# Ten of the sixteen k tiles of an input projection by Strassen's scheme, ahead of the rest

## The chip, the cores and the metric

The kernel runs on one core of a Trainium2 chip. Its engines work side by side: TensorE (PE) multiplies matrices into PSUM, VectorE (DVE) and ScalarE (ACT) do elementwise work and read PSUM, GpSimd (POOL) does elementwise work in SBUF alone, SyncE (SP) issues most of the DMAs. The metric is the device time of one execution in microseconds (us).

## The reference

One decoder layer for a prompt of 1024 tokens and 8 samples of one token each, all in float32:

```python
h = rmsnorm(x, g_norm) * (1 + scale) + shift        # shift, scale, gate from silu(c) @ w_ada
p = h @ w_in                                        # 2048 -> 5 * 1024 + 8 + 3 * 1024
q, k, v, o, z_ml, i_pre, f_pre, u, v_cm, z_cm = split(p)
h_ml = rmsnorm(sigmoid(o) * mlstm(q, k, v, i_pre, f_pre)) * silu(z_ml)      # 4 heads of 256, chunks of 128 tokens
h_cm = gelu(u) * spatial_mix(layernorm(gelu(v_cm))) * silu(z_cm)            # 4 groups of 256
y = rmsnorm(x + gate * (concat(h_ml, h_cm) @ w_out), g_final)
```

Outputs are y for prompt and samples, the new matrix memories, normalisers and maxima, and the normalised v rows of the samples.

## The kernel before

The 1024 tokens are worked in two halves of 512. The input projection (2048 features in, 16 k tiles of 128) is cut into 32 sections of 256 columns: eight keys (k, v, q, o, z, vc, u, zc) for each of four heads j, so that every section runs once in each half. Each float32 operand is split into a high and a low part, and a product takes three matmuls: high by high, low by high, high by low. `wsplit` (L318) splits the weights, a cast on ACT (L324) and a subtraction on DVE (L325), a piece of two k tiles at a time; it does so in each half anew. `section` (L395) runs the matmuls: with tokens on the PSUM partitions for v, o and vc (L426, L427, L429, 256 columns), with features on the partitions for the others (L437, L440; 512 columns in the second half, 256 and 264 in the first, where the samples' eight columns ride behind the tokens). In the first half the samples' part of v, o and vc is a product of its own (`sample_mm`, L334).

`take` (L367) loads the weight pieces, one `stream` of pieces planned in order (`plan`, L377), some pieces ahead into a ring of three `raw` buffers, and splits them into rings of four. Work that needs no place of its own (the samples' gates, state update and output `s_out` L1112, the ada gate, the first half's `finish` L824) is cut into steps; `run` (L454) puts one step after every second piece of a section, four to a section. The steps of `s_out` load w_out again in pieces of 512 KB (L1134) and multiply them by the samples' rows (L1136). `fold_x` (L808) adds x and the gate to the second half's sums in steps, behind the last vc section; what is left of the background steps is drawn there first, ahead of the u of the last head (L1337 to L1339).

The order within an engine is the program's where `late` (the framework's hold) stands; elsewhere the framework's scheduler orders the instructions by its own model of when they are ready. Each engine then executes its list in order.

At the start the ada weights of 256 features at a time (`ada_pair`, L152), x of the first half (L1219) and the pieces of k, v and q come in turns, so that the first three sections grow k tile by k tile (L1246 to L1275). h of the second half is prepared beside the last section of the first. Of a head: k is evicted and transposed (`ml_k`, L568, transposes L581), then v, q, the chunk recurrence `ml_chain` (L623), o, z, `ml_post` (L659), vc, the output projection of the head (`out_proj`, L797), u, zc.

## Time and profile before

| | |
|---|---|
| median of 3 runs | 2187.31 us (2184.13 to 2187.61) |
| span of the profiled execution, first to last instruction | 2186.8 us |
| PE busy with matmuls | 2125.5 us (97%), 14290 instructions |
| DVE / ACT / POOL busy | 1052.9 / 694.3 / 283.6 us |
| moved by DMA | 307.84 MB, mean 141 GB/s |

The profiled execution has no time of its own beside its span; the span lies 0.5 us below the median of the runs. A busy time counts the duration of instructions; matmuls overlap their successors, so a matmul's duration is longer than what it adds to the time, and prices are better read from start to start. In the rows of instructions in order of time, the columns are start, duration, engine, line, output and inputs, count; a bracket at the end gives the idle time ahead of the instruction and what ended it.

### The profile page before, as it was taken

The page shows a single profiled execution, that of the slowest core. Times are in us where ns is not written, and L with a number is a line of the kernel's source. Part 1 is how long each engine was busy: PE and PEld are TensorE (multiplying, and loading weights), DVE is VectorE, ACT ScalarE, POOL GpSimd, SP SyncE. Part 2 cuts the span into 40 slices and gives each one's busy share as a digit, 9 for nine tenths or more (in the row PEclk, how much of TensorE's full clock was granted, in tenths as well). Part 3 has the DMA queues.
Part 4 walks back from the last instruction along what each step waited for, and adds up shares of the span by engine and source line. Part 5 has one row for each costly group of instructions (what it writes and reads, how often), then busy time and mean ns, then how long its engine had stood idle before and what let it go on. Part 6 is the DMA issues. An engine that isn't in the chain of part 4 may idle for free. (4 is left out here: it accounts for less than half of the span.)

```text
span 2186.8 us, 35645 instructions
## 1 busy us (share of the span) xinstructions
PE 2125.5 (97%) x14290; PEld 1823.1 (83%) x14290; DVE 1052.9 (48%) x2078; ACT 694.3 (32%) x1342; POOL 283.6 (13%) x322
## 2 busy tenths in 40 slices
PE   5999999999999999999999999999999999999996
PEld 3778898888988989889978898788888787788985
DVE  4344634325343354433556556655754335344396
ACT  2233232223223423223262353333332232322324
POOL 1100010000100000000040551100010000001064
PEclk8999999999999999999999999999999999999998
DMA  9962343444535433222342454565563353544343
GB/s 335 323 203 71 109 149 113 135 139 129 153 111 177 129 99 97 79 68 84 100 144 79 143 168 134 165 182 167 182 188 102 118 159 112 168 135 120 92 149 122
DMA packets 280550, 307.84 MB, mean 141 GB/s; under 512 B 16160, under 2 KB 250800, under 8 KB 279872
## 3 DMA queue, kind: packets, MB, share of 16 engines
q1 hardware_dynamic: 276288, 296.49, 44.2%
...
q8 instruction: 112, 1.84, 0.3%
...
HBM read 285.18 MB, written 20.32 MB: 140 GB/s over the span
## 5 line engine op out<-in xcount | busy, mean ns | idle before, releaser
L325 DVE TENSOR_TENSOR wlo<-raw,whi 128x512 fp32r<-128x512 f32 x634 | 458.8, 729 | 901.1 <-ACT whi L324 347.1
L324 ACT CAST whi<-raw 128x512 fp32r<-128x512 f32 x634 | 385.2, 620 | 1234.3 <-PE pp L440 370.8
L437 PE MATMUL pp<-hhi,whi 128*128 128x256 f32 (+1 forms) x1856 | 518.1, 330 | 0.4 <-DVE hhi L258 0.4
L440 PE MATMUL pp<-hlo,whi 128*128 128x256 f32 (+1 forms) x1856 | 509.4, 325 | 0.4 <-DVE hlo L263 0.4
L426 PE MATMUL pp<-whi,hhi 128*128 128x256 f32 x1536 | 380.4, 287 | 0.0
L427 PE MATMUL pp<-whi,hlo 128*128 128x256 f32 x1536 | 372.7, 281 | 0.0
L437 PEld LDWEIGHTS pp<-hhi,whi 128*128 128x128 f32 x1856 | 310.3, 188 | 63.7 <-issue 28.5
L437 PE MATMUL pp<-hhi,wlo 128*128 128x256 f32 (+1 forms) x1856 | 352.9, 324 | 0.0
L440 PEld LDWEIGHTS pp<-hlo,whi 128*128 128x128 f32 x1856 | 310.7, 188 | 30.4 <-issue 0.8
L426 PEld LDWEIGHTS pp<-whi,hhi 128*128 128x128 f32 x1536 | 290.6, 189 | 24.6 <-issue 22.2
L437 PEld LDWEIGHTS pp<-hhi,wlo 128*128 128x128 f32 x1856 | 279.6, 188 | 32.2 <-issue 0.8
L427 PEld LDWEIGHTS pp<-whi,hlo 128*128 128x128 f32 x1536 | 290.4, 189 | 0.8 <-issue 0.4
L429 PE MATMUL pp<-wlo,hhi 128*128 128x256 f32 x1536 | 213.6, 282 | 0.0
L791 PE MATMUL pp<-whi,g 128*128 128x512 f32 x488 | 193.9, 397 | 5.0 <-ACT g L687 5.0
L429 PEld LDWEIGHTS pp<-wlo,hhi 128*128 128x128 f32 x1536 | 195.1, 189 | 0.0
L792 PE MATMUL pp<-whi,g 128*128 128x512 f32 x488 | 192.9, 395 | 0.2 <-DVE g L689 0.2
L806 DVE TENSOR_TENSOR yacc<-yacc,pp 128x512 f32<-128x512 f32 x204 | 136.3, 684 | 41.8 <-PE pp L794 41.5
L794 PE MATMUL pp<-wlo,g 128*128 128x512 f32 x488 | 154.0, 396 | 1.1 <-DVE wlo L325 1.0
L791 PEld LDWEIGHTS pp<-whi,g 128*128 128x128 f32 x488 | 92.0, 189 | 27.8 <-ACT g L687 5.8
L794 PEld LDWEIGHTS pp<-wlo,g 128*128 128x128 f32 x488 | 92.1, 189 | 23.4 <-DVE wlo L325 2.1
L792 PEld LDWEIGHTS pp<-whi,g 128*128 128x128 f32 x488 | 92.0, 189 | 21.1 <-DVE g L689 0.5
L819 POOL TENSOR_TENSOR yacc<-yacc,xl 128x512 f32<-128x512 f32 x32 | 53.4, 1683 | 77.3 <-DVE yacc L818 76.5
...
## 6 DMA issues: line engine op xcount, KB each, us to landing
raw<-in_w_in_dram SPq DMA_DIRECT2D x256, 512.0 KB
...
```

What stands on the lines that cost most here:

```text
L324: hold(A.copy(hi, raw))
L325: hold(V.tensor_tensor(out=lo, in0=raw, in1=hi.bitcast(F32), op=ALU.subtract))
L426: pin(T.matmul(o, hhi[kt][:, tk], hi, start=(st and tt % 2 == 0), stop=False, skip_group_check=True))
L427: pin(T.matmul(o, hlo[kt][:, tk], hi, start=False, stop=False, skip_group_check=True))
L429: pin(T.matmul(o, hhi[kt][:, tk], lo, start=False, stop=en, skip_group_check=True))
L437: pin(T.matmul(o, w[:, fk], hhi[kt][:, tk], start=so, stop=en, skip_group_check=True))
L440: pin(T.matmul(o, hi[:, fk], hlo[kt][:, tk], start=False, stop=False, skip_group_check=True))
L791: T.matmul(po, hc[a][0][:, tk], sp_[a][0][:, 0, :], start=(start and a == 0), stop=False)
L792: T.matmul(po, hc[a][1][:, tk], sp_[a][0][:, 0, :], start=False, stop=False)
L794: T.matmul(po, hc[a][0][:, tk], sp_[a][1][:, 0, :], start=False, stop=(a == 1 and not more))
L806: V.tensor_tensor(out=yv, in0=yv, in1=po, op=ALU.add)
L819: G.tensor_tensor(out=yv, in0=yv, in1=xl[:, t2, :], op=ALU.add)
```

## The change

For 10 of the 16 k tiles the input projection is now done first, for all 1024 tokens, by the Strassen-Winograd scheme. A block is two k tiles by two halves of the tokens (four parts of h) and two halves of a section's columns (four parts of the weights). Seven products of sums of these parts replace eight products of the parts. `combos` forms the seven operands of h of a block, each split into high and low; `Seven` forms the weight operands of a section (four sums on POOL), splits them and runs the products into four PSUM banks, which ACT, DVE and POOL add up to the four output parts. This runs in two stretches over all 32 sections: stretch 1 with blocks 0 and 1 (4 k tiles), stretch 2 with blocks 2 to 4 (6 k tiles). The sums go to DRAM (`spool`), stretch 2 reads those of stretch 1 and adds to them. In the background of stretch 1 h of blocks 2 to 4 is prepared, in that of stretch 2 the ada weights of blocks 5 to 7, h of the first half of them, and the ada gate.

Then the halves run as before over the 6 k tiles that are left, all sections with features on partitions; `part` loads the sums of a section from DRAM (512 KB) and DVE adds them when it evicts PSUM. `tokens` turns v, o and vc on TensorE. The samples' products for the 10 k tiles run in stretches 1 and 2, two sections at a time (`sample_two`); for the 6 others they ride behind the tokens in all sections of the first half. Weight pieces of the halves are half as large (one piece of two k tiles, or one k tile of w_out), six loads are in flight and three pieces split ahead. A section now has three pieces, and a background step follows each. `s_out` takes its pieces from the ring `part`. At the start x is read whole, all eight token tiles, and the ada weights of blocks 0 and 1 follow. Buffers are opened and closed by phase. The diff, cut to its core:

```diff
-SPLIT = ["v0", "v1", "v2", "v3", "o0", "o1", "o2", "o3", "vc0", "vc1", "vc2", "vc3", "k0", "q0"]
+KEYS = ("k", "v", "q", "o", "z", "vc", "u", "zc")
+SECS = [(key, j) for j in range(NH) for key in KEYS]
+SUBS = [(0, 2), (2, 3)]
+K2 = 2 * sum(n for _, n in SUBS)
+KN = KT - K2
...
+    spool = [[dr.tile([P, 2048], F32, name=f"spool{n}_{i}") for i in range(len(SECS))] for n in range(len(SUBS))]
+    psd = [dr.tile([P, len(SECS) * 256], F32, name=f"psd{n}") for n in range(len(SUBS))]
...
+    def combos(at, hf, eng):
+        a11, a21, a12, a22 = hf
+        def put(n, t):
+            A.copy(at[:, n, :], t)
+            V.tensor_tensor(out=at[:, 7 + n, :], in0=t, in1=at[:, n, :].bitcast(F32), op=ALU.subtract)
+        put(0, a11)
+        put(1, a12)
+        put(2, a22)
+        yield
+        t1, t2 = s2(), s2()
+        V.tensor_tensor(out=t1, in0=a21, in1=a22, op=ALU.add)
+        eng.tensor_tensor(out=t2, in0=t1, in1=a11, op=ALU.subtract)
+        put(3, t1)
+        put(4, t2)
+        yield
+        t3 = s2()
+        V.tensor_tensor(out=t3, in0=a12, in1=t2, op=ALU.subtract)
+        put(6, t3)
+        yield
+        t4 = s2()
+        eng.tensor_tensor(out=t4, in0=a11, in1=a21, op=ALU.subtract)
+        put(5, t4)
+        yield
+    def slot(pool):
+        return pool.tile([P, 14, 512], F32R, tag="as", name=nm("as"), bufs=3 if pool is pl["big"] else 1)
+    class Seven:
+        def __init__(self, sub, n):
+            self.sub, self.n = sub, n
+            b0, self.nb = SUBS[sub]
+            key, j = SECS[n]
+            c0 = SEC[key] + j * 256
+            self.raw = pl["big"].tile([P, 2 * self.nb, 256], F32, tag="raw", name=nm("raw"), bufs=2)
+            S.dma_start(self.raw, win[:, 2 * b0:2 * b0 + 2 * self.nb, c0:c0 + 256])
+            self.co = None
+        def load_co(self):
+            self.co = cot()
+            if self.sub:
+                S.dma_start(self.co.rearrange("p a b -> p (a b)"), spool[self.sub - 1][self.n])
+        def sums(self):
+            r = self.raw.rearrange("p (b i) (n c) -> p b i n c", i=2, n=2)
+            b11, b12, b21, b22 = r[:, :, 0, 0, :], r[:, :, 0, 1, :], r[:, :, 1, 0, :], r[:, :, 1, 1, :]
+            t = [pl["big"].tile([P, self.nb, P], F32, tag="t", name=nm("t"), bufs=4) for _ in range(4)]
+            sub = lambda o, a, b: G.tensor_tensor(out=o, in0=a, in1=b, op=ALU.subtract)
+            sub(t[0], b12, b11)
+            sub(t[1], b22, t[0])
+            sub(t[2], b22, b12)
+            sub(t[3], t[1], b21)
+            self.prod = [(b11, 0, 0), (t[1], 4, 1), (b21, 1, 0), (t[0], 3, 2), (t[2], 5, 1), (b22, 6, 2), (t[3], 2, 3)]
+            self.hl = {}
+        def split(self, m):
+            w = self.prod[m][0]
+            hi, lo = (pl["big"].tile([P, self.nb, P], F32R, tag=t, name=nm(t), bufs=4) for t in ("hi", "lo"))
+            A.copy(hi, w)
+            V.tensor_tensor(out=lo, in0=w, in1=hi.bitcast(F32), op=ALU.subtract)
+            self.hl[m] = (hi, lo)
+        def product(self, m, at):
+            _, place, bank = self.prod[m]
+            if m == 0:
+                self.ps = [None] * 4
+            first = self.ps[bank] is None
+            if first:
+                self.ps[bank] = psb()
+            o = self.ps[bank]
+            hi, lo = self.hl.pop(m)
+            nb = self.nb
+            for b in range(nb):
+                for n, (w, d) in enumerate(((hi, 0), (hi, 7), (lo, 0))):
+                    T.matmul(o, w[:, b, :], at[b][:, place + d, :], start=(first and b == 0 and n == 0), stop=(b == nb - 1 and n == 2), skip_group_check=True)
+            x, y, z, v = self.ps
+            co = self.co
+            c11, c21, c12, c22 = co[:, 0, 0:512], co[:, 0, 512:], co[:, 1, 0:512], co[:, 1, 512:]
+            add = lambda e, o, a, b, op=ALU.add: e.tensor_tensor(out=o, in0=a, in1=b, op=op)
+            half = lambda t: pl["big"].tile([P, 512], F32, tag=t, name=nm(t), bufs=2 if t == "pa" else 1)
+            if m == 0:
+                self.a = half("pa")
+                A.copy(self.a, x)
+            elif m == 1:
+                self.u = half("pu")
+                add(V, self.u, self.a, y)
+                if self.sub:
+                    add(G, c12, c12, self.u)
+            elif m == 2:
+                if self.sub:
+                    add(V, c11, c11, x)
+                else:
+                    A.copy(c11, x)
+            elif m == 3:
+                if self.sub:
+                    add(V, c22, c22, z)
+                else:
+                    A.copy(c22, z)
+            elif m == 4:
+                add(V, self.a, self.a, y)
+                if self.sub:
+                    add(G, c21, c21, self.a)
+                add(V if self.sub else G, c22, c22, self.a)
+            elif m == 5:
+                add(V, c12, c12 if self.sub else self.u, z)
             else:
+                add(V, c21, c21 if self.sub else self.a, v, ALU.subtract)
+        def store(self):
+            S.dma_start(spool[self.sub][self.n], self.co.rearrange("p a b -> p (a b)"))
+    def sample_two(sa, sb):
+        ps = psb()
+        b0, nb = SUBS[sa.sub]
+        nk = 2 * nb
+        for i in range(nk):
+            j = i % 4
+            for n, s in enumerate((sa, sb)):
+                T.matmul(ps[32 * j:32 * j + 32, 256 * n:256 * n + 256], hs[:, 2 * b0 + i, :], s.raw[:, i, :],
+                         start=(i < 4 and n == 0), stop=(i + 4 >= nk), tile_position=(0, 32 * j), skip_group_check=True)
+        e = s2()
+        A.copy(e, ps)
+        S.dma_start(psd[sa.sub][:, sa.n * 256:sa.n * 256 + 512], e)
+    def sub_phase(sub, at, bg):
+        secs = {}
+        def get(n):
+            if n < len(SECS) and n not in secs:
+                secs[n] = Seven(sub, n)
+        AHEAD = 3
+        get(0)
+        get(1)
+        secs[0].sums()
+        for m in range(AHEAD):
+            secs[0].split(m)
+        for n in range(len(SECS)):
+            s = secs[n]
+            s.load_co()
+            for m in range(7):
+                if m == 3 and n + 1 < len(SECS):
+                    secs[n + 1].sums()
+                g = m + AHEAD
+                if g < 7:
+                    s.split(g)
+                elif n + 1 < len(SECS):
+                    secs[n + 1].split(g - 7)
+                if m == 1 and n % 2 == 0:
+                    sample_two(s, secs[n + 1])
+                s.product(m, at)
+                next(bg, None)
+            s.store()
+            get(n + 2)
+            del secs[n]
...
+    def part(key, h, half):
+        if (key, h, half) not in parts:
+            t = pl["wp"].tile([P, 2, 512], F32, tag="part", name=nm("part"), bufs=2)
+            late(S.dma_start(t, spool[-1][SECS.index((key, h))].rearrange("p (f t) -> p f t", f=2)[:, :, half * 512:half * 512 + 512]))
+            parts[key, h, half] = t
+        return parts[key, h, half]
+    def section(key, h, half):
+        samples = half == 0
         pt = [psb(), psb()]
+        hv = hh[half]
+        fm = part(key, h, half)
+        if samples:
+            acc = psb()
+            cols = [[(pt[0][:, 0:256], slice(0, 256)), (pt[1][:, 0:256 + NB], slice(256, HALF + NB))],
+                    [(pt[0][:, 256:512], slice(0, 256)), (acc[:, 0:256 + NB], slice(256, HALF + NB))]]
         else:
+            cols = [[(pt[ft], slice(0, HALF))] for ft in range(2)]
+        for q in range(KN // 2):
+            hi2, lo2 = take("s", key, h, q, half)
+            for ps_ in range(2):
+                for g in range(2):
+                    kt = 2 * q + g
+                    hi, lo = hi2[:, g, :], lo2[:, g, :]
+                    st, en = (kt == 0 and ps_ == 0), (kt == KN - 1 and ps_ == 1)
+                    for ft in range(2):
+                        fk = slice(ft * P, ft * P + P)
+                        for n, (o, tk) in enumerate(cols[ft]):
+                            so = st and not (samples and n == 0 and ft == 1)
+                            w = hi if ps_ == 0 else lo
+                            T.matmul(o, w[:, fk], hv[:, kt, 0, tk], start=so, stop=en, skip_group_check=True)
+                        if ps_ == 0:
+                            for o, tk in cols[ft]:
+                                T.matmul(o, hi[:, fk], hv[:, kt, 1, tk], start=False, stop=False, skip_group_check=True)
+            if q < KN // 2 - 1:
+                yield None
+        n = SECS.index((key, h)) + 1
+        if half == 0 or n < len(SECS):
+            part(*SECS[n % len(SECS)], half + n // len(SECS))
+        if samples:
+            collect(key, h, [cols[ft][1][0][:, 256:] for ft in range(2)])
+        ts = []
+        for ft in range(2):
+            t = g2([P, 512])
+            for o, tk in cols[ft]:
+                tk = slice(tk.start, min(tk.stop, HALF))
+                V.tensor_tensor(out=t[:, tk], in0=o[:, 0:tk.stop - tk.start], in1=fm[:, ft, tk], op=ALU.add)
+            ts.append(t)
+        yield ts
...
+    def tokens(ts):
+        pt = [psb(), psb()]
+        for tt in range(4):
+            for ft in range(2):
+                c = (tt % 2) * 256 + ft * P
+                T.transpose(pt[tt // 2][:, c:c + P], ts[ft][:, tt * P:tt * P + P], ident)
+        return pt
...
-    def run(key, h, token_major, half, mid=None):
-        for i, r in enumerate(section(key, h, token_major, half == 0)):
-            if i == 3 and mid is not None:
-                mid()
-            if i % 2 == 1:
-                next(bgq[0], None)
+    def run(key, h, half):
+        for r in section(key, h, half):
+            next(bgq[0], None)
         return r
...
-                    raw = wp.tile([P, 4, 256], F32, tag="raw", name=nm("raw"), bufs=3)
+                    raw = pl["wp"].tile([P, 4, 256], F32, tag="part", name=nm("raw"), bufs=2)
...
     def back_a():
         yield from s_gates()
-        for key in ("k", "v", "q"):
-            yield from sample_only(key, 0)
-        for n in range(4):
-            yield from ada_gate(n)
-        part = sm([P, 4, 4])
-        for tt in range(4):
-            for n in range(2):
-                xl = wp.tile([P, 1024], F32, tag="xl", name=nm("xl"), bufs=2)
-                late(S.dma_start(xl, xp[:, 4 + tt, n * 1024:n * 1024 + 1024]))
-                yield
-                for i in range(2):
-                    late(A.activation(xl[:, i * 512:i * 512 + 512], xl[:, i * 512:i * 512 + 512], AF.Square, accum_out=part[:, tt, 2 * n + i:2 * n + i + 1]))
-        rstdB[0] = rstd_rows(part)
-        yield
+        yield from h_second(1, G)
...
+    at = []
+    for blk in range(SUBS[0][1]):
+        for _ in ada_pair(blk, True):
+            pass
+        hf = hf_tile()
+        for _ in h_block(blk, lambda tt: xk[:, tt, blk * 256:blk * 256 + 256], [0, 1], hf):
+            pass
+        at.append(slot(pl["s1" if blk else "big"]))
+        for _ in combos(at[-1], hf, V):
+            pass
+    nxt = {}
+    def bg_a():
+        b0, nb = SUBS[1]
+        for blk in range(b0, b0 + nb):
+            yield from ada_pair(blk)
+        for blk in range(b0, b0 + nb):
+            xl = [load_x(blk, 0), load_x(blk, 1)]
+            yield
+            nxt["hf"] = hf_tile()
+            yield from h_block(blk, lambda tt: xl[tt // 4][:, tt % 4, :], [0, 1], nxt["hf"])
+            if blk < b0 + nb - 1:
+                t = slot(pl["big"])
+                nxt[blk] = t
+                yield from combos(t, nxt["hf"], G)
+    def bg_b():
+        for blk in range(K2 // 2, 8):
+            yield from ada_pair(blk)
+        yield from h_second(0, V)
         for n in range(4):
+            yield from ada_gate(n)
+    bg = bg_a()
+    sub_phase(0, at, bg)
+    for _ in bg:
+        pass
+    close_pool("s1")
+    open_pool("hh0", "left")
+    b0, nb = SUBS[1]
+    t = slot(pl["big"])
+    for _ in combos(t, nxt["hf"], V):
+        pass
+    bg = bg_b()
+    sub_phase(1, [nxt[b] for b in range(b0, b0 + nb - 1)] + [t], bg)
+    for _ in bg:
+        pass
+    close_pool("pre")
+    open_pool("w2", "left")
...
+            ks = run("k", j, half)
             if half == 0 and j == 0:
                 def front():
                     yield from gates(0)
+                for _ in front():
                     pass
                 bgq[0] = back_a()
+            k, ktok = ml_k(ks)
+            if pend is not None:
+                out_proj(*pend, half)
+                pend = None
+            v = ml_v(tokens(run("v", j, half)))
+            gt = gst["gt"]
+            Pm = w_intra(j, gt)
+            q = run("q", j, half)
+            num = ml_chain(half, j, k, ktok, v, q, Pm, gt)
+            o = ml_o(tokens(run("o", j, half)))
+            z = ml_z(run("z", j, half), j)
+            hc = ml_post(j, num, o, z, gt)
+            y = cm_v(tokens(run("vc", j, half)))
             out_proj(ya, 2 * j, hc, half, first=(j == 0), ns=3 + (j < 3 or half == 0))
             hml = hc
             m = cm_mix(j, y)
...
                 if half:
                     bgq[0] = fold_x(ya, half)
                     next(bgq[0])
+            cm_u(run("u", j, half), m)
...
```

## Rows read from the trace of the kernel before

**Rows 1.** the page's busy line and its 40 slices of PE, in tenths

```profile
PE 2125.5 (97%) x14290; PEld 1823.1 (83%) x14290; DVE 1052.9 (48%) x2078; ACT 694.3 (32%) x1342; POOL 283.6 (13%) x322
...
PE   5999999999999999999999999999999999999996
```

**Rows 2.** waits of PE: who waited for whom; us in total, times, longest

```profile
PE pp L252 <- DVE x_a L1259: 11.1, 1, 11.1
...
PE pp L581 <- ACT g L573: 3.6, 4, 2.0
```

**Rows 3.** busy time by stretch: length, engines busy, granted clock, DMA share, GB/s

```profile
40.00:50.00 10.00, 9.06 (x71) 5.50 (x64) 9.13 (x29) 0.63 (x2) 0.72 (x1) 1.00 1.09 375
300.00:1100.00 800.00, 795.48 (x6122) 720.09 (x6121) 327.46 (x605) 231.14 (x466) 50.06 (x66) 1.00 0.39 117
1150.00:2100.00 950.00, 937.64 (x5403) 792.65 (x5402) 494.58 (x1018) 311.54 (x564) 127.00 (x141) 0.99 0.47 140
```

**Rows 4.** PE in order of time: start, us, line; ends of two pieces

```profile
1502.20 0.28 PE L426 MATMUL pp<-whi,hhi 128*128 128x256 f32 x1
...
1505.05 0.28 PE L426 MATMUL pp<-whi,hhi 128*128 128x256 f32 x1
...
1507.85 0.40 PE L437 MATMUL pp<-hhi,whi 128*128 128x512 f32 x1
...
1510.63 0.40 PE L437 MATMUL pp<-hhi,whi 128*128 128x512 f32 x1
```

**Rows 5.** PE in order of time, from 1688 us: transposes, section, s_out

```profile
1688.48 1.16 PE L1124 MATMUL pp<-ident,g 8*128 8x8 f32 x16
1689.56 0.39 PE L426 MATMUL pp<-whi,hhi 128*128 128x256 f32 x1
...
1690.38 0.28 PE L426 MATMUL pp<-whi,hhi 128*128 128x256 f32 x1
1690.59 0.64 PE L1136 MATMUL pp<-raw,hs 128*32 128x256 f32 x8
1691.16 0.39 PE L427 MATMUL pp<-whi,hlo 128*128 128x256 f32 x1
```

**Rows 6.** PE in order of time, from 1288 us: eight transposes, next section

```profile
1288.66 1.03 PE L680 MATMUL pp<-ident,g 128*128 128x128 f32 x8
1289.45 0.37 PE L426 MATMUL pp<-whi,hhi 128*128 128x256 f32 x1
```

**Rows 7.** PE in order of time: the first product of the input projection

```profile
40.67 0.50 PE L437 MATMUL pp<-hhi,whi 128*128 128x512 f32 x1 [0.38 <-DVE hhi L258]
```

**Rows 8.** groups by line, DVE and POOL, shapes apart: busy us, mean ns

```profile
L806 DVE TENSOR_TENSOR yacc<-yacc,pp 128x512 f32<-128x512 f32 x204 | 136.3, 684 | 41.8 <-PE pp L794 41.5
L1069 DVE SCALAR_TENSOR_TENSOR r<-xl,g 128x256 f32<-128x256 f32 x64 | 23.8, 425 | 11.8 <-DMA g<-psf 6.1 <-DMA g<-psa 5.5
...
L648 POOL TENSOR_SCALAR r<-g,s 128x257 f32<-128x257 f32 x32 | 31.5, 994 | 229.4 <-PE pp L642 120.0 <-ACT g L601 53.2 <-DVE r L1069 42.8
L263 POOL TENSOR_TENSOR hlo<-g,hhi 128x512 fp32r<-128x512 f32 x16 | 20.8, 1325 | 17.6 <-ACT hhi L260 17.6
```

**Rows 9.** POOL and DVE in order of time, from 1270 us

```profile
1270.00 10.37 POOL L836 TENSOR_TENSOR yacc<-yacc,gt 128x512 f32<-128x512 f32 x7 [1.22 <-ACT yacc L835]
...
1271.69 3.31 DVE L325 TENSOR_TENSOR wlo<-raw,whi 128x512 fp32r<-128x512 f32 x2
```

**Rows 10.** DVE in order of time: products of s_state with q

```profile
1520.10 0.43 DVE L1069 SCALAR_TENSOR_TENSOR r<-xl,g 128x256 f32<-128x256 f32 x1 [4.14 <-DMA g<-psf]
```

**Rows 11.** SP, ACT, PE in order of time: load, first use, s_out's end

```profile
1703.36 0.37 SPq L353 DMA_DIRECT2D raw<-in_w_in_dram  x1
...
1707.54 0.62 ACT L324 CAST whi<-raw 128x512 fp32r<-128x512 f32 x1 [1.36 <-DMA raw<-in_w_in_dram]
...
1969.11 0.64 PE L1136 MATMUL pp<-raw,hs 128*32 128x256 f32 x8
```

656 lines of the change are left out of this document (242 added, 414 removed).

## The prediction

> **What bounds the kernel now.** I read the page's busy line and its slices first [rows 1]: TensorE (PE) is busy 97% of the span, in all slices but the first and the last; VectorE (DVE) 48%. The waits of PE say the same [rows 2]: the longest is 11.1 us at the start, and the transposes of k behind their eviction wait 3.6 us in all. So the time is the sum of PE's instructions at the pace at which they issue, plus a start and an end. The windows [rows 3] give the slack: in 300 to 1100 us, at full clock, PE is busy 99.4% with DVE at 41%; in 1150 to 2100 us 98.7% with DVE at 52%. Matmul durations overlap, so a matmul is priced from start to start [rows 4]: 24 of 256 columns take 2.85 us (0.1188 each), 12 of 512 columns 2.78 us (0.2317).
>
> **The matmuls of the input projection.** Removed: 24 token-major sections of 192 x 0.1188 = 547; 18 sections of the first half with the samples' columns, 192 x 0.1188 = 411; 22 feature-major ones of 96 x 0.2317 = 489; sum 1447 us. Added: stretch 1 (4 k tiles), 32 sections x 7 products x 2 blocks x 3 x 0.2317 = 311; stretch 2 (6 k tiles) 32 x 7 x 3 x 3 x 0.2317 = 467; the 6 k tiles left over, first half 32 x 72 x 0.1188 = 274, second half 32 x 36 x 0.2317 = 267; sum 1319. Net -128 us: 102 from seven products for eight (32 sections x 5 blocks x 1536 columns at 2.4 GHz), the rest from 512-column matmuls and fewer sample columns.
>
> **PE work that is added.** Sample matmuls rise from 448 to 640 instructions; 8 take 0.57 us [rows 5], so 192 x 0.071 = +14. sample_two puts two sections on one column group in succession; if that costs the overlap between groups, up to +36. v, o and vc now come with features on partitions and are turned by tokens(): 24 x 8 = 192 transposes; 8 take 0.79 us [rows 6], +19. PE's net so far: -95 us.
>
> **The start: +15 (0 to +35).** Before, the first product starts at 40.67 us [rows 7], and from 40 to 50 us PE is at 91% with the DMAs at 375 GB/s [rows 3]. Now all 8 MB of x and the ada weights of two blocks (8 MB) come ahead of the first product: 16 MB at that rate is 43 us, behind about 7 us of small loads. Then come transposes, the first combinations (eleven DVE instructions of about 0.68 [rows 8]) and their waits, some 15 us: about 65 us. PE does about 10 us more useful work before that point than it did, hence +15.
>
> **Joints: +18 (5 to 35).** The fifth block's combinations take the buffer of a block of stretch 1 and can't be written before that stretch ends: +6. Where the halves begin, w_s is loaded and turned at once, and gates(0) is run to its end behind the first k section, where the o and z sections covered it before: +12.
>
> **Waits for evictions: +12 (0 to 36).** tokens() waits for two DVE additions of 0.68 [rows 8], where the transposes of k waited for one ScalarE copy, up to 2.0 us [rows 2]. I take 24 x 0.5, since PE does take later matmuls first: seven of the next piece stand ahead of s_out's L1136 while its transposed rows are copied [rows 5]. Without that, 24 x 1.5.
>
> **DVE and GpSimd in stretches 1 and 2: +25 (10 to 60).** By section in stretch 1: seven splits of 256 elements (0.42, as L1069) and four additions from PSUM (0.68, as L806) make 5.7 us on DVE; on GpSimd four sums of 256 (0.74, scaled down from L263's 1.33 for 512) and one of 512 make 4.3 [rows 8]. Stretch 2: 7 x 0.56 + 7 x 0.68 = 8.7 on DVE, 4 x 1.0 + 2 x 1.3 = 6.6 on GpSimd. The two get in each other's way [rows 9]: while seven GpSimd instructions ran in 10.37 us, two DVE subtractions took 3.31 us in place of 1.4, so 58% of GpSimd's time was lost to DVE. With that DVE needs 8.2 of PE's 10.3 us in stretch 1 (9.73 + 0.57 of samples) and 12.6 of 15.5 in stretch 2: 80%, where the trace of before knows 41 and 52%. PE's idle share doubled between those two (0.6 to 1.3%); carried on it is about 3% of 820 us. The ada loads fall in the same place: 12 MB in the first eight sections through three buffers beside 1 MB stores, some 340 of the 375 GB/s; that is in the same +25. Below +10 I don't go: nothing here shortens PE's stream.
>
> **DVE in the halves: +20 (5 to 55).** Second half: 52% of 987 us is 514; 160 splits go (-110), 64 additions of the partial sums come (+44), q and the turned k move to others (-11): 437 us of DVE in 547 us of PE, 80%. The steps beside the sections come every 2.8 us of PE and not every 5.6, so s_state has half the lead; already before, DVE once waited 4.14 us for its rows [rows 10]. 3% of 547, and a little for the first half.
>
> **What is left of s_out: +45 (10 to 100).** Before, a section takes four background steps, 120 in the 30 sections up to vc of the last head; about 109 are wanted, and L1136 ends at 1969 us [rows 11], in the last head's v section. Now a section has three yields: 90 steps for about 112. Two of s_out's four column blocks, 16 loads of 512 KB, are drained ahead of u. They share the ring "part" (2 buffers) with the sections. A load takes 4.2 us from issue to first use [rows 11]; with its matmuls and its issue 5.2, or 2.6 with two in flight: 2 x 5.2 + 14 x 2.6 = 47 us, covered by u, zc, the head of the last projection and their own matmuls (31): +16. fold_x stands behind it: 16 GpSimd additions of 1.5 us [rows 9], 24 in all, of which some 15 no longer find cover. The 20 loads ahead of the drain go one by one through a ring that is also the sections': 104 us for 67 us of steps; two output projections absorb most: +14. Lower end: the drain is covered; upper: PE waits through it.
>
> **Sum.** 2186.8 - 95 + 15 + 18 + 12 + 25 + 20 + 45 = 2227. The profiled span lies 0.5 us under the median of the runs, so I take 2227 for both.
>
> **Rivals.**
> Covered (not slower), chance 0.36. The mechanism is the place of s_out's remainder. If u, zc and the last projection's head are placed ahead of it and two loads stay in flight, it costs 10, not 45, and DVE, less held up by late instructions, leaves PE idle in the four stretches half as much (-40 on the waits above): 2227 - 35 - 40 = 2152 (2100 to 2183). It decides from where PE's idle time past the start stays under some 60 us. For it: the two long windows of before hold only 17 us of PE idle time in 1750 [rows 3]. Against: the rings are half as deep in time.
> Shared port (slower), chance 0.12. If DVE loses all of GpSimd's time, not 58%, it needs 9.9 of 10.3 us and 15.3 of 15.5; background (30 us of DVE work in the first eight sections) goes on top and DVE sets the pace: about 1 us for each of 64 sections, 65 in place of 25: 2267. It decides as soon as a sum of 256 elements takes the 0.99 us of L648 [rows 8] and not 0.74. The Trainium skill, SBUF — State Buffer, section "Who interferes with whom", says that a VectorE instruction with two SBUF inputs and a GpSimd instruction that reads SBUF shut each other out for a whole instruction; by that rule this rival's 9.9 and 15.3 us hold. The rows show 58%, so the trace bears the rule out in kind, not in full size.
> That the change doesn't do what it says, eight products for seven, would give back 102 us; the seven are written out in the code, so I give it no chance.
>
> **How the numbers follow.** Forecast 2227 (2190 to 2290) 0.52; covered 0.36; shared port 0.12. The range for 8 in 10 goes from 2130 (most of the covered case) to 2305 (the upper ends of the waits, but not all at once); both signs lie in it, and 2190 to 2290 is the forecast's own. A measurement here can tell about 0.2% from no change, 4.4 us; the edges of both cases put 0.06 within it. Faster 0.36, slower 0.58.
>
> **What would show it.** Products at 0.232 us a matmul, 42 and 63 a section; the first product near 65 us; DVE at 75 to 85% in the windows of stretches 1 and 2; the rest of s_out in a bunch behind the last vc, with a DMA as releaser and PE idle. It would be wrong if PE were idle for under 60 us past the start (covered), or if sections took 11.5 and 16.5 us with DVE over 95% (shared port).

## The result, and the profile after

The changed kernel takes 2378.38 us (median of 4 runs, 2373.05 to 2381.0), the kernel before 2187.46 beside it: the ratio is 1.0869 (interval 1.0852 to 1.0886). The change costs 191 us. The sign of the forecast was right; the time, 151 us above it, lies outside the range. The profiled execution has a span of 2376.7 us, 189.9 more than before.

The page of the kernel after, busy line, three of the rows by slice, and the granted clock:

```profile
PE 2089.5 (88%) x11315; PEld 1635.5 (69%) x11315; DVE 1422.4 (60%) x2765; ACT 793.5 (33%) x1592; POOL 637.7 (27%) x650
...
PE   2999999999999999979999999987977976998455
...
DVE  3566555656456665556656575676866775744247
...
PEclk9999999999999999989999999999998988999667
```

TensorE is still near 100% through two thirds of the span and holes come only afterwards, where before all slices but the first and last were full [rows 1]. The clock row falls with them: what is lost at the end is lost twice, once standing and once at the lower of TensorE's two levels.

Busy time by stretch in the kernel after (length, busy us of PE, PEld, DVE, ACT, POOL, granted clock, DMA share, GB/s): before the first product, stretch 1, stretch 2, the joint, the rest of the first half, the second half up to the last background steps, their drain, the tail:

```profile
40.00:50.00 10.00, 5.42 (x52) 3.56 (x56) 2.75 (x7) 2.04 (x8) 1.46 (x4) 1.00 0.97 314
76.00:450.00 374.00, 367.42 (x1901) 271.14 (x1899) 219.18 (x430) 168.63 (x373) 152.08 (x163) 1.00 0.56 190
450.00:996.00 546.00, 546.00 (x2908) 402.38 (x2907) 321.75 (x511) 152.53 (x292) 238.10 (x193) 1.00 0.67 232
996.00:1046.00 50.00, 29.85 (x215) 26.65 (x213) 21.17 (x65) 8.62 (x19) 2.06 (x6) 0.76 0.42 127
1046.00:1566.00 520.00, 506.62 (x3345) 456.34 (x3344) 325.19 (x678) 188.83 (x376) 59.10 (x70) 1.00 0.37 112
1566.00:2210.00 644.00, 534.48 (x2407) 415.35 (x2408) 423.39 (x901) 215.17 (x402) 114.24 (x132) 0.91 0.54 156
2210.00:2285.00 75.00, 21.41 (x144) 4.51 (x142) 6.40 (x10) 3.99 (x8) 2.94 (x2) 0.54 0.40 128
2285.00:2377.00 92.00, 57.17 (x198) 41.68 (x196) 73.31 (x83) 28.92 (x61) 55.28 (x48) 0.76 0.41 135
```

Strassen's stretches are the best part of the kernel: TensorE is busy for all 546 us of the second one. The second half has 110 us without a busy TensorE where the windows of before had 5 and 12 [rows 3]; the drain has 54, the tail 35.

The longest waits of TensorE in the kernel after (us in total, times, longest), to be held against [rows 2]:

```profile
PE pp L1271 <- DMA raw<-in_w_out_dram: 65.8, 22, 7.6
PE pp L231 <- DVE xsb L228: 39.6, 1, 39.6
PE pp L813 <- DVE g L808: 33.5, 5, 14.1
PE pp L724 <- DVE g L607: 26.0, 6, 11.7
PE pp L617 <- DVE g L607: 15.3, 21, 2.8
```

L1271 are the products of s_out, L231 belongs to the start, L813 are the transposes of ml_post, L724 those of k, L617 those of tokens(); L607 is the new eviction with the partial sums.

The difference of the two spans, from the busy lines and the idle times ahead of TensorE's instructions. The cost of the low clock is an estimate: in windows of 5 us, TensorE's busy time times one less the granted clock, summed.

| | before | after | difference |
|---|---|---|---|
| busy, less the next line | 2116 | 2034 | -82 |
| by the low clock | 9 | 55 | +46 |
| TensorE idle | 49 | 277 | +228 |
| the rest (behind the last matmul) | 12 | 11 | -2 |
| span | 2186.8 | 2376.7 | +190 |

### The profile page after: what moved, and what is told of

It reads as the page before. It is cut to its first block, busy times and chain, and to the rows that moved or that the text cites. A ratio compares the mean times of both kernels' runs of the same rounds, so it can differ in the third digit from the quotient of the medians.

```text
span 2376.7 us, 31911 instructions
## 1 busy us (share of the span) xinstructions
PE 2089.5 (88%) x11315; PEld 1635.5 (69%) x11315; DVE 1422.4 (60%) x2765; ACT 793.5 (33%) x1592; POOL 637.7 (27%) x650
## 5 line engine op out<-in xcount | busy, mean ns | idle before, releaser
L351 PE MATMUL pp<-as,hi 128*128 128x512 f32 x2240 | 711.4, 398 | 2.9 <-ACT pa L359 2.9
L351 PEld LDWEIGHTS pp<-as,hi 128*128 128x128 f32 x2240 | 410.5, 188 | 137.8 <-issue 24.2
L351 PE MATMUL pp<-as,lo 128*128 128x512 f32 x1120 | 438.2, 391 | 0.0
L499 ACT CAST whi<-raw 128x512 fp32r<-128x512 f32 x314 | 188.2, 618 | 512.2 <-PE pp L594 208.6
L591 PE MATMUL pp<-hh,whi 128*128 128x256 f32 (+2 forms) x1152 | 317.9, 330 | 0.0
L500 DVE TENSOR_TENSOR wlo<-raw,whi 128x512 fp32r<-128x512 f32 x314 | 224.5, 723 | 149.5 <-PE pp L591 72.4
L594 PE MATMUL pp<-hh,whi 128*128 128x256 f32 (+2 forms) x1152 | 312.4, 325 | 0.0
L351 PEld LDWEIGHTS pp<-as,lo 128*128 128x128 f32 x1120 | 210.3, 188 | 48.4 <-DVE pa L355 0.4
L591 PE MATMUL pp<-hh,wlo 128*128 128x256 f32 (+2 forms) x1152 | 216.6, 324 | 4.2 <-DVE wlo L500 4.2
L591 PEld LDWEIGHTS pp<-hh,whi 128*128 128x128 f32 x1152 | 196.1, 192 | 22.5 <-issue 6.6
L594 PEld LDWEIGHTS pp<-hh,whi 128*128 128x128 f32 x1152 | 195.1, 192 | 15.9 <-issue 0.4
L591 PEld LDWEIGHTS pp<-hh,wlo 128*128 128x128 f32 x1152 | 173.2, 191 | 23.2 <-DVE wlo L500 5.1
L336 DVE TENSOR_TENSOR lo<-t,hi 128x256 fp32r<-128x256 f32 (+1 forms) x256 | 129.3, 506 | 76.4 <-ACT hi L335 76.4
L607 DVE TENSOR_TENSOR g<-pp,part 128x256 f32<-128x256 f32 (+1 forms) x192 | 86.7, 506 | 83.9 <-PE pp L591 81.3
```

What stands on the lines that cost most here:

```text
L336: V.tensor_tensor(out=lo, in0=w, in1=hi.bitcast(F32), op=ALU.subtract)
L351: T.matmul(o, w[:, b, :], at[b][:, place + d, :], start=(first and b == 0 and n == 0), stop=(b == nb - 1 and n == 2), skip_group_check=True)
L499: A.copy(hi, raw)
L500: V.tensor_tensor(out=lo, in0=raw, in1=hi.bitcast(F32), op=ALU.subtract)
L591: T.matmul(o, w[:, fk], hv[:, kt, 0, tk], start=so, stop=en, skip_group_check=True)
L594: T.matmul(o, hi[:, fk], hv[:, kt, 1, tk], start=False, stop=False, skip_group_check=True)
```

## The experiments

Two theories stood at the beginning. A: VectorE, whose list runs in order, is held up by the background's instructions and by the rows they wait for, and TensorE waits for what stands behind them. B: a section of 8.4 us is too short to cover the way from its eviction to the transposes that use it. Others (D, E, L and T) came up as runs decided against parts of these; each is put in words where it is tested.

A head of the second half is the unit of most readings. It runs from the first transpose of k to that of the next head, the last one to the end of the last section; in brackets are the idle times ahead of TensorE's instructions that start in it, summed. In the first half of the kernel after a head without much background (j = 1) takes 137 us (3).

| kernel | time | j = 0 | j = 1 | j = 2 | j = 3 | behind |
|---|---|---|---|---|---|---|
| before | 2187 | 245 (4) | 250 (6) | 267 (2) | 217 (1) | 49 |
| after | 2378 | 173 (24) | 169 (32) | 168 (38) | 221 (68) | 72 |
| e1, no s_state | 2322 | 176 (25) | 138 (15) | 143 (8) | 219 (65) | 72 |
| e5, s_state without loads | 2352 | 172 (23) | 152 (21) | 158 (22) | 219 (65) | 73 |
| e3, ring of four | 2319 | 167 (23) | 163 (22) | 168 (34) | 172 (20) | 71 |
| e4, new order | 2354 | 168 (26) | 158 (20) | 162 (21) | 200 (67) | 74 |
| e11, no finish | 2345 | 146 (6) | 164 (27) | 163 (34) | 224 (67) | 71 |
| e13, no sums | 2324 | 163 (18) | 165 (21) | 167 (36) | 185 (32) | 70 |
| e9, 8 k tiles | 2361 | 206 (42) | 194 (26) | 205 (27) | 166 (16) | 53 |
| e17, before, cut | 1914 | 182 (21) | 192 (29) | 180 (9) | 140 (2) | 65 |

**The drain of s_out: e3.**

```diff
-            t = pl["wp"].tile([P, 2, 512], F32, tag="part", name=nm("part"), bufs=2)
+            t = pl["wp"].tile([P, 2, 512], F32, tag="part", name=nm("part"), bufs=4)
...
-                    raw = pl["wp"].tile([P, 4, 256], F32, tag="part", name=nm("raw"), bufs=2)
+                    raw = pl["wp"].tile([P, 4, 256], F32, tag="part", name=nm("raw"), bufs=4)
```

> The ring part has four buffers and not two, for the sections and s_out alike. If the 16 loads of s_out behind the last vc section run one at a time (4.65 us each) since the next section's part holds the second buffer, three are now in flight, one comes each 1.6 us, the drain of 75 us falls to about 28, and some of the loads ahead of it leave TensorE alone: about 2325 us. If the DMA engines set those 4.65 us (512 KB at 110 GB/s), nothing changes: 2378 us.

2318.66 us (1.0611 of before, 1.0595 to 1.0627), 60 us less. TensorE in order of time during the drain of the kernel after (start, us, line, tile, count, idle time ahead and its releaser):

```profile
2220.68 1.08 PE L1271 MATMUL pp<-raw,hs 128*32 128x256 f32 x8 [3.57 <-DMA raw<-in_w_out_dram]
2225.36 1.08 PE L1271 MATMUL pp<-raw,hs 128*32 128x256 f32 x8 [3.60 <-DMA raw<-in_w_out_dram]
```

The loads of these pieces, as SP issues them, in the same kernel:

```profile
2221.82 0.38 SPq L1269 DMA_DIRECT2D raw<-in_w_out_dram  x1
2226.50 0.37 SPq L1269 DMA_DIRECT2D raw<-in_w_out_dram  x1
```

TensorE in e3:

```profile
2209.24 1.08 PE L1271 MATMUL pp<-raw,hs 128*32 128x256 f32 x8 [1.29 <-DMA raw<-in_w_out_dram]
2211.59 1.08 PE L1271 MATMUL pp<-raw,hs 128*32 128x256 f32 x8 [1.26 <-DMA raw<-in_w_out_dram]
2213.09 1.08 PE L1271 MATMUL pp<-raw,hs 128*32 128x256 f32 x8 [0.42 <-DMA raw<-in_w_out_dram]
```

In the kernel after the pieces come 4.7 us apart. Each load is issued only when the matmuls of the piece before are done (they end at 2221.76 us, the issue is at 2221.82): one buffer of the two holds the next section's sums. With four buffers they come 1.4 to 3.3 us apart, and head j = 3 falls from 221 to 172 us. The DMA engines were not the bound.

**s_state left out, and its loads alone: e1, e5, e2.** In e1 empty steps stand for the sixteen updates:

```diff
-                g1 = s_state(b, hp_, decb)
...
+        for _ in range(34):
+            yield
```

> Left out: the samples' state update s_state (its loads, its products on VectorE, its stores), with the same number of empty background steps in its place. Theory A (VectorE runs the background's instructions in its list ahead of the evictions, and stands still where their rows have not landed): TensorE's idle time from 1735 to 2075 us falls from 67 to about 25 us, and with it most of the 11 us that the low clock costs there: about 2328 us. Theory B (in the second half a section is 8.4 us of TensorE, too short to cover the way from its eviction to the transposes that use it, with or without s_state): the stalls ahead of L724 and L813 stay at 8 us and more each, the time falls by 15 at most: 2363 us or above.

2321.68 us (1.0627, 1.0611 to 1.0643): 57 less, where theory A said 50. Heads j = 1 and 2, in which the updates ran, fall to 138 and 143 us, close to the 137 of the first half. Theory B had them keep their stalls. In e5 the updates stay and use fixed rows and one fixed state:

```diff
-        Ct = pl["wp"].tile([P, 4, HD], F32, tag="xl", name=nm("xl"), bufs=2)
-        late(S.dma_start(Ct, state_C[0, b, 2 * hp_:2 * hp_ + 2].rearrange("h (a p) d -> p (h a) d", p=P)))
+        if b == 0 and hp_ == 0:
+            C0 = pl["wp"].tile([P, 4, HD], F32, tag="c0", name="c0", bufs=1)
...
+        C0, qb, kb = sv["c0"], sv["q0"], sv["k0"]
```

> Left out: s_state's loads; all sixteen updates use the first one's rows and state from fixed buffers, its work on VectorE and ScalarE and its stores stay. If s_state costs its 57 us because VectorE stands still for rows that have not landed (41 us of it ahead of L1204 from 1700 to 2120 us), nearly all of it comes back: 2335 us or less. If it is VectorE's work itself (64 us in a half in which VectorE is busy for 70% anyway), the time falls by 15 at most: 2363 us or above.

2352.01 us (1.0765, 1.0744 to 1.0785), between the two answers: 26 of the 57 us go with the loads, for which VectorE stood still, and some 30 stay with the rest of the updates, their work on VectorE and ScalarE and their stores. In e2 the loads come a step earlier, three updates in flight:

```diff
-        late(S.dma_start(Ct, state_C[0, b, 2 * hp_:2 * hp_ + 2].rearrange("h (a p) d -> p (h a) d", p=P)))
         qb, kb = g2([P, 512]), g2([P, 512])
...
+        Ct = pl["wp"].tile([P, 4, HD], F32, tag="xl", name=nm("xl"), bufs=4)
+        late(S.dma_start(Ct, state_C[0, b, 2 * hp_:2 * hp_ + 2].rearrange("h (a p) d -> p (h a) d", p=P)))
+        yield
```

> s_state asks for its rows ahead of the 512 KB of state, uses them two background steps later and not one, and four xl buffers stand in place of two; its work on VectorE stays. If it is the wait for the rows that holds VectorE (31 us ahead of L1204 in the second half), most of theory A's gain is had: 2340 to 2350 us. If it is the work itself (64 us of VectorE) or the short sections (theory B): 2365 to 2380 us.

2369.8 us (1.0847, 1.0829 to 1.0865), 9 less. VectorE's waits ahead of these products fall from 41 to 19 us only (now for the state, no longer for the rows), so this run alone would not have told the two apart.

What a stall looks like, in the kernel after, head j = 1: VectorE in order of time around the end of the z section.

```profile
1821.14 0.43 DVE L1204 SCALAR_TENSOR_TENSOR r<-xl,g 128x256 f32<-128x256 f32 x1 [6.67 <-DMA g<-psa]
...
1824.53 1.28 DVE L607 TENSOR_TENSOR g<-pp,part 128x512 f32<-128x512 f32 x2
...
1828.69 1.41 DVE L752 SCALAR_TENSOR_TENSOR g<-g,pfm,g 128x512 f32<-128x512 f32 x2
...
1832.04 1.15 DVE L808 TENSOR_SCALAR g<-g,s 128x256 f32<-128x256 f32 x4 [0.94 <-POOL s L153]
```

TensorE in order of time in the same stretch of the same kernel:

```profile
1820.03 1.09 PE L591 MATMUL pp<-hh,wlo 128*128 128x512 f32 x4
1832.45 2.12 PE L813 MATMUL pp<-ident,g 128*128 128x128 f32 x8 [11.33 <-DVE g L808]
1834.22 0.78 PE L591 MATMUL pp<-hh,whi 128*128 128x512 f32 x1
1834.79 0.63 PE L594 MATMUL pp<-hh,whi 128*128 128x512 f32 x1
...
1838.56 0.40 PE L591 MATMUL pp<-hh,whi 128*128 128x512 f32 x1
1838.79 0.40 PE L594 MATMUL pp<-hh,whi 128*128 128x512 f32 x1
```

VectorE stood 6.67 us for the rows of an update, and then worked off its list in order: updates, splits, the eviction, ml_post. TensorE ended its section at 1821.1 us, and the next instructions of its list, the transposes of ml_post (L813), needed L808, which came last of all these: 11.33 us. The matmuls behind the stall start 0.43 us apart, those from 1838.56 on 0.23: the rows show 512 columns at 1.2 and at 2.4 GHz.

**The order of the program: e4.**

```diff
-            k, ktok = ml_k(ks)
             if pend is not None:
                 out_proj(*pend, half)
                 pend = None
+            k, ktok = ml_k(ks)
...
-            hc = ml_post(j, num, o, z, gt)
-            y = cm_v(tokens(run("vc", j, half)))
+            post = ml_post(j, num, o, z, gt)
+            next(post)
+            ys = run("vc", j, half)
+            hc = next(post)
+            y = cm_v(tokens(ys))
```

(v behind q and o behind z in the same way.)

> Program order alone: the last output projection stands ahead of the transposes of k, the q section ahead of those of v, the z section ahead of those of o, the vc section ahead of ml_post's transposes. Theory B: each eviction then has a section or a projection (8 to 11 us) to cover it; the waits ahead of L724, L617 and L813 (69 us in the second half, 11 us more by the clock) go for the most part: about 2310 us. Theory A: VectorE's list is as late as before, the idle time moves to the next matmul that needs it, and the time stays above 2355 us.

2353.9 us (1.0777, 1.0761 to 1.0793), 24 less. That is 1 us under the 2355 above which theory A put it, and 44 above theory B's 2310. The waits ahead of the transposes of k are gone, others grow in their place.

**The first half's finish left out: e11.**

```diff
-                    yield from finish(ya, 0)
+                    for _ in range(13):
+                        yield
```

> Left out: the first half's finish (adding x and the gate, its norm, its output), with empty steps in its place. The head j = 0 of the second half takes 173 us, the heads j = 1 and 2 without s_state took 138 and 143. If GpSimd's list (16 additions and 16 products of 512 elements) holds the small powers and scalings of the head behind it (releasers POOL ahead of L784, L808), this head falls to about 145 us: 2350 us. If the gates at its start are the cause: 173 stays, 2375 us.

2344.67 us (1.0726, 1.0703 to 1.075), 34 less; head j = 0 falls from 173 (24) to 146 (6). So finish is to this head what s_state is to the next two.

**Work taken from VectorE: e7, e12, e13.** In e7 the split's subtraction goes to GpSimd in the second half:

```diff
-        V.tensor_tensor(out=lo, in0=raw, in1=hi.bitcast(F32), op=ALU.subtract)
+        (G if d[-1] == 1 else V).tensor_tensor(out=lo, in0=raw, in1=hi.bitcast(F32), op=ALU.subtract)
```

> In the second half the subtraction of the weights' split goes to GpSimd (160 instructions, 110 us of VectorE, 213 of GpSimd at 1.33). If VectorE's load is what makes the second half's evictions late, its busy share there falls from 70 to some 55% and the idle time of its four heads (94 us, 35 more by the clock) by half: about 2315 us. If GpSimd takes the same time away from VectorE again, or the split pieces come too late for TensorE, nothing is won: 2375 us or above.

2409.01 us (1.1024, 1.1003 to 1.1046), 31 more. A subtraction takes 1.32 us on GpSimd where VectorE took 0.72 on the mean, and TensorE's waits ahead of ml_post's transposes (L813) grow from 33.5 to 45.8 us. In e12 and e13 the eviction leaves VectorE's list:

```diff
+                if half == 1 and key in ("k", "v", "o", "vc"):
+                    A.copy(t[:, tk], o[:, 0:tk.stop - tk.start])
+                    G.tensor_tensor(out=t[:, tk], in0=t[:, tk], in1=fm[:, ft, tk], op=ALU.add)
```

> In the second half k, v, o and vc leave PSUM by a ScalarE copy and get their partial sums on GpSimd; VectorE no longer stands between these sections and their transposes. Theory D (the change moved the evictions from ScalarE into VectorE's list, which the background holds up; before, VectorE was held up as well and nobody waited for it): the waits ahead of L724 and L617 (36 us) and part of the low clock go: about 2335 us. If the path is as long with GpSimd (0.6 + 1.3 us each, and its own list), or the head is held by VectorE at other places all the same: 2370 us or above.

2403.16 us (1.0998, 1.098 to 1.1017), 25 more. TensorE now waits for GpSimd in the same places:

```profile
PE pp L728 <- POOL g L609: 32.1, 6, 12.7
PE pp L621 <- POOL g L609: 30.9, 18, 4.6
```

```diff
+                if half == 1:
+                    A.copy(t[:, tk], o[:, 0:tk.stop - tk.start])
```

> Left out: the addition of the partial sums in the second half; ScalarE copies every section from PSUM as it did before the change (32 x 2 copies), the loads of the sums stay. Theory D: without VectorE on this path the idle time of the second half's first three heads falls from 94 to some 45 us and the low clock with it: about 2310 us. If only VectorE's load counts (44 us of additions less), 20 us at most: 2358 us.

2324.17 us (1.063, 1.0614 to 1.0646), 54 less, but not where theory D put it: the first three heads win 15 us together, their idle time falls from 94 to 75, not to 45. 36 us come from head j = 3. There the sums are loaded and nobody reads them, so that the ring is free for s_out as in e3: TensorE's waits for pieces of w_out fall from 65.8 to 27.0 us. That reading was not tried by itself. Of the loss in the first three heads the eviction in VectorE's list is a small part.

**Section length, and the pace of the steps: e9, e14, e15.**

```diff
-SUBS = [(0, 2), (2, 3)]
+SUBS = [(0, 2), (2, 2)]
...
-            raw = pl["w2"].tile([P, 2, 256], F32, tag="raw", name=nm("raw"), bufs=6)
+            raw = pl["w2"].tile([P, 2, 256], F32, tag="raw", name=nm("raw"), bufs=3)
```

> 8 of 16 k tiles by Strassen's scheme and not 10 (stretch 2 with two blocks, not three); to make room, three raw buffers and not six. TensorE's work by the rows' pace: stretch 2 loses 32 x 7 x 3 x 0.232 = 156 us, the halves win 32 x 24 x 0.119 + 32 x 12 x 0.232 = 180: +24. A section of the halves is 11.2 us and not 8.4, with four background steps and not three. If short sections with few steps are what costs the second half its time, the drain of s_out goes (-60) and half of the other stalls (-45): about 2300 us, less matrix work saved and yet faster. If only the number of steps counts: 2340. If the second half's loss hangs on the work beside it and not on the sections: 2400 us.

2360.96 us (1.0801, 1.0785 to 1.0817). The drain is gone (head j = 3 and what is behind it: 219 us in place of 293), the first three heads are hardly better: 95 us idle where it was 94. The waits for s_out's pieces have moved into them, 18.5 us of the 95 where it was 2.9 of 94:

```profile
PE pp L1271 <- DMA raw<-in_w_out_dram: 19.5, 12, 6.5
```

(This line counts the whole span of e9.) Without them 76 us are left of 91: longer sections with more steps to each helped little. (The three raw buffers may have cost something in all of this run.) For the pace of the steps alone, e14 leaves out finish and s_out, and e15 also every third step:

```diff
-        for r in section(key, h, half):
-            next(bgq[0], None)
+        for i, r in enumerate(section(key, h, half)):
+            if half == 0 or i != 1:
+                next(bgq[0], None)
```

> Left out: the first half's finish and the whole of s_out, with no empty steps in their place; s_state comes 13 steps earlier. From the runs without finish (34 us) and with a ring of four (60) and the products of s_out (some 20): 2265 us. It is there to be compared with the next one.

> The same work left out, and in the second half two background steps to a section in place of three. Theory E (the steps, 2.8 us of TensorE apart where they were 5.6 apart before, come faster than a state's load, products and store can follow, so that VectorE and ScalarE stand in their lists): the updates come farther apart, VectorE waits less for rows, TensorE's idle time beside the sixteen updates (50 us) falls by 20 to 30, the time to about 2240 us. If it is the updates' work that costs the time, at whatever pace: 2265 us, as the one before, or more for what is left to drain.

2217.09 us (1.0127, 1.0109 to 1.0146) and 2225.02 (1.0174, 1.0157 to 1.0191). e14 comes 48 us under its forecast: what it leaves out was worth more than the runs that touched one part of it had shown. The updates run from 1704 to 1918 us beside 36 us of idle TensorE in e14, from 1755 to 2055 beside 38 in e15. VectorE waits less for rows (11 against 21 us), as theory E said, and nothing is won: the idle time beside an update, 2.3 us on the mean, is the same at either pace. (It holds what these heads would stand idle without the updates, too.) Theory E fell.

**The kernel before with less matrix work: e17.** 8 of the 16 k tiles are left out in its second half:

```diff
-                    yield from (("s", key, j, kq, half) for kq in range(4))
+                    yield from (("s", key, j, kq, half) for kq in range(2 if half else 4))
...
-            if i % 2 == 1:
+            if i % 2 == 1 or half == 1:
                 next(bgq[0], None)
```

> The kernel before, with 8 of the 16 k tiles left out of the second half's input projection, so that its sections take 11.2 us as in the run with 8 k tiles by Strassen's scheme (e9), with a background step after every piece, four to a section, as there. No partial sums are added, v, o and vc still come with tokens on the partitions, and ScalarE evicts as before. By the rows' pace 32 x 11.2 = 360 us of TensorE go: 1826 us if nothing else changes. Theory L (the background beside too little matrix work, whatever the evictions are): the first three heads of the second half stand as still as e9's, 95 us and some 20 by the clock: about 1930 us. Theory T (the sums, evictions and transposes that the change put on VectorE's path): these heads stay below 25 us of idle time, 1850 us at most.

1913.52 us (0.8757, 0.8742 to 0.8771), between the two forecasts: of 360 us of matmuls taken away only 273 come back. Its windows over the heads j = 0 and 1 of the second half (columns as above):

```profile
1152.00:1334.00 182.00, 160.68 (x821) 135.87 (x821) 131.32 (x263) 78.96 (x156) 75.67 (x76) 0.92 0.44 129
1334.00:1527.00 193.00, 159.36 (x817) 134.56 (x817) 129.29 (x328) 68.46 (x123) 16.58 (x21) 0.90 0.69 191
```

Its longest waits of TensorE, of the whole span:

```profile
PE pp L681 <- DVE g L676: 19.5, 1, 19.5
PE pp L632 <- DVE g L593: 13.4, 6, 7.5
```

VectorE in order of time while TensorE stands those 19.5 us, from 1426.4 to 1446.0 us, ahead of ml_post's transposes:

```profile
1429.33 0.43 DVE L1070 SCALAR_TENSOR_TENSOR r<-xl,g 128x256 f32<-128x256 f32 x1 [4.29 <-DMA g<-psf]
...
1440.91 0.43 DVE L1070 SCALAR_TENSOR_TENSOR r<-xl,g 128x256 f32<-128x256 f32 x1 [4.22 <-DMA g<-psa]
```

TensorE is idle for 59 us in the first three heads (12 before the cut), VectorE is busy for 72 and 67%, and the clock falls to 0.92 and 0.90: the picture of the kernel after, down to the waits for an update's rows, with no line of the change in it. So theory L holds for the larger part: e9, with the same section length, has 95 us there, and 59 come with the cut alone. Of the 36 between them 18 are e9's waits for s_out's pieces in the ring that they share with the sums (0.9 us in e17, which has another ring); if the parts simply add, some 18 are left for the evictions by VectorE, the transposes and the loads of the sums. The cut also brings the background steps closer together in time; e14 and e15 show no cost of the pace as such.

**The tail: e6, e18.**

```diff
-                    G.tensor_tensor(out=yv, in0=yv, in1=xl[:, t2, :], op=ALU.add)
+                    (G if part is not None else V).tensor_tensor(out=yv, in0=yv, in1=xl[:, t2, :], op=ALU.add)
```

> In the second half fold_x adds x on VectorE and no longer on GpSimd (16 additions, 24 us of GpSimd in the tail). If GpSimd holds up VectorE's instructions with two SBUF inputs there (1.75 us and not 0.69 for L500, L523, L904 from 2301 to 2333 us), VectorE wins some 15 us and pays 11: the tail of 72 us behind the last section falls by 5 to 10, 2370 us. If VectorE's own list is what bounds the tail, it grows by those 11: 2388 us.

2364.67 us (1.0823, 1.0806 to 1.0839), 14 less. 6 of them lie behind the last section (72 to 66 us), where the moved additions are; where the others come from was not looked into. VectorE's groups in the tail of the kernel after (count, busy us, mean ns):

```profile
L950 DVE TENSOR_TENSOR yacc<-yacc,gt 128x512 f32<-128x512 f32 x16 | 16.8, 1103 | 0.0
...
L500 DVE TENSOR_TENSOR wlo<-raw,whi 128x512 fp32r<-128x512 f32 x6 | 8.3, 1393 | 0.1
...
L523 DVE TENSOR_TENSOR raw<-raw,gt 128x512 f32<-128x512 f32 x4 | 7.3, 1834 | 0.0
```

The same in e6:

```profile
L951 DVE TENSOR_TENSOR yacc<-yacc,xl 128x512 f32<-128x512 f32 x16 | 10.8, 684 | 2.8 <-DMA xl<-in_x_prompt_dram 2.8
L950 DVE TENSOR_TENSOR yacc<-yacc,gt 128x512 f32<-128x512 f32 x16 | 10.6, 678 | 0.0
...
L500 DVE TENSOR_TENSOR wlo<-raw,whi 128x512 fp32r<-128x512 f32 x6 | 5.1, 860 | 3.5 <-ACT whi L499 3.5
...
L523 DVE TENSOR_TENSOR raw<-raw,gt 128x512 f32<-128x512 f32 x4 | 2.7, 679 | 0.1
```

VectorE takes over 10.8 us and its own instructions shrink by more: without GpSimd's additions beside them they take 0.68 us (L500 0.86) on the mean, not 1.1 to 1.8. The same edit needs nothing of the change, so it was tried in the kernel before:

> The kernel before with fold_x's second half on VectorE, the one edit that helped the changed kernel and does not need the change. In the tail of the kernel before TensorE stands still twice, 2.1 and 2.9 us, behind L773, which takes 2.07 us beside GpSimd's additions and 0.69 alone: some 3 us of 2187 come back, and a little of the low clock behind them. If VectorE's 11 us more of work in its last 100 us are late elsewhere: no change or 5 us more.

2182.61 us, 0.9983 of before (0.9974 to 0.9992): 4 us, the only version here that does all of the work and is faster than the kernel before.

**The gains together: e8, e10, e16.** e8 is e3, e4 and e7 in one, e10 is e3, e4 and e6, e16 is e10 with fold_x on VectorE in both halves.

> The ring of four, the new order and the subtraction on GpSimd in one kernel. If the three causes are separate, their gains add up: 60 and 25 us, and what the subtraction alone brings: 2294 us less that. If they are the same idle time seen from three sides, the time stays above 2305 us.

> The ring of four, the new order and fold_x on VectorE together. If their gains (60, 25 and 14 us) are separate causes: 2280 us. If the new order wins only idle time that the other two win as well: 2305 us.

> The ring of four, the new order, and fold_x on VectorE in both halves and not in the second alone. If GpSimd's list is what holds the head j = 0 (finish costs it 27 us there), 16 additions of 1.45 us leave it for 11 us of VectorE: 2275 us. If VectorE has no room there: 2290 us or above.

2320.73 us (1.0619, 1.0603 to 1.0635), 2288.89 (1.0468, 1.0452 to 1.0483) and 2283.34 (1.0434, 1.042 to 1.045). The gains, with e7's loss of 31 us in e8, add up to within some 10 us, so the causes are separate ones; e16 lies between its two forecasts; together they win back 95 of the 191 us, and no version with the change that does all of the work reaches the kernel before.

## Why the prediction was wrong, point by point

| term of the sum | predicted | measured |
|---|---|---|
| matmuls, samples, transposes | -95 | -82 |
| start | +15 | +29 |
| joints | +18 | +26 |
| evictions; VectorE in stretches 1 and 2; VectorE in the halves | 12 + 25 + 20 | stretches and first half +12, second half +119 |
| what is left of s_out, with fold_x behind it | +45 | drain +63, tail +26 |
| behind the last matmul | - | -2 |

(Measured are the idle times of the stage with the low clock's cost, less those of before: 23 and 2 us at its start, 8 together from there to the second half, 12 and 4 in that half, 5 and 3 in its tail.)

**The matrix work held**, to 13 us, which were not traced. Where no background work runs beside it, a section takes what the sum said, 9.7 us and 10.9 with the samples' products (10.3 on the mean) in stretch 1, 14.3 and 16.4 in stretch 2. (While the background has matmuls of its own there, a section of stretch 2 takes up to 21.5 us, with no idle time of TensorE.) The stores of the sections' sums, which SP issues in order, show it:

```profile
315.47 0.32 SPq L386 DMA_DIRECT2D spool<-co  x1
325.19 0.32 SPq L386 DMA_DIRECT2D spool<-co  x1
336.10 0.32 SPq L386 DMA_DIRECT2D spool<-co  x1
...
921.75 0.32 SPq L386 DMA_DIRECT2D spool<-co  x1
936.03 0.32 SPq L386 DMA_DIRECT2D spool<-co  x1
952.44 0.32 SPq L386 DMA_DIRECT2D spool<-co  x1
```

**The stretches were priced too high.** The step took 58% of all of GpSimd's time from VectorE, whatever VectorE did. The trace of stretch 2 has the loss on instructions with two inputs in SBUF alone, and only where GpSimd runs beside them; groups of VectorE in the kernel after, 700 to 950 us:

```profile
L355 DVE TENSOR_TENSOR co<-co,pp 128x512 f32<-128x512 f32 x65 | 44.5, 684 | 28.1 <-PE pp L351 28.1
L336 DVE TENSOR_TENSOR lo<-t,hi 128x384 fp32r<-128x384 f32 x65 | 36.0, 554 | 18.8 <-ACT hi L335 18.8
L336 DVE TENSOR_TENSOR lo<-raw,hi 128x384 fp32r<-128x384 f32 x49 | 30.6, 624 | 0.0
L355 DVE TENSOR_TENSOR co<-co,pa 128x512 f32<-128x512 f32 x17 | 30.3, 1782 | 0.0
```

Additions that read PSUM and one tile of SBUF keep their 0.684 us, though GpSimd runs beside most of them; the one that reads two tiles of SBUF, always while GpSimd adds, takes 1.782, as the tail's do in e6's comparison. The subtractions of the splits (L336) also read two tiles of SBUF, but more than half of them run while GpSimd stands, and they stay at 0.554 and 0.624 us on the mean, where the prediction had 0.56. VectorE was busy 59% of both stretches (219 of 374 and 322 of 546 us), not 80%, and the shared-port rival charged GpSimd's time to instructions that the trace shows untouched. The Trainium skill, SBUF — State Buffer, section "Who interferes with whom", also says that a VectorE instruction with at most one SBUF input, outside its two-port modes, doesn't contend. The trace agrees (0.684 us), and that half of the rule was left out of the working. In the tail a tensor_scalar with one input in SBUF (L851) is slowed as well: 1.48 us, where it takes 0.41 in e6.

**The start and the joints** were of the right kind and too small: the first product comes at 76.4 us, not 65, since x and the ada weights came at 314 GB/s in a window that had 375 before [rows 3] (259 on the mean from 0 to 76 us), and the joint to the halves costs 20 us idle and 6 by the clock. The joint between the stretches, priced at 6, costs nothing.

**The step that failed is "VectorE in the halves, +20".** It carried on TensorE's idle share by VectorE's busy share, to 3% at 80%. In the second half VectorE is busy for 66% (423 of 644 us) and TensorE idle for 17%; in the stretches it is busy for 59% and TensorE idle for none in the second; in the first half, at 63% (325 of 520), for 3%. The share is no measure of it. What decides is, for the larger part, shown by e17: the work beside the matrix products in the second half (finish, the sixteen updates, s_out, each head's own chain) runs through lists that execute in order, and before, 938 us of busy TensorE lay over it from 1150 to 2100 us [rows 3]. After, it is 534 from 1566 to 2210: the change took some 400 us of matrix work from this stage, and little of what lies beneath. Beside the sixteen updates TensorE was idle for 6 us before (1376 to 1627 us) and is for 52 after (1804 to 2050). So each piece shows up in the time when it is taken out: s_state 57 us, finish 34, and the drain 60 by its ring. The prediction saw that s_state has half the lead, priced this and the rest of the halves together at 20 us, where the second half alone cost 119, and has no term for finish.

**s_out** was the right mechanism with a wrong term: its 47 us of loads counted two in flight; there was one, and u, zc and the projection that should have covered 31 us were not pulled ahead.

**The low clock** is in no term. In the long windows of before the granted clock was 0.99 and 1.00 [rows 3]; with 228 us more of idle time, much of it in pieces of 3 to 14 us, the low level costs some 46 us more.

**The rivals.** Covered was right on the stretches and wrong on the rest; its point, 60 us of idle time past the start, was passed by 167. That the seven products give back their 102 us was rightly given no chance: the sections run at the length that seven products need.

Open is why the idle time beside an update does not depend on the pace, and how the last 18 us or so between e9 and e17 divide over evictions, transposes and loads of the sums.
